# Letting the first output store of a batched matrix product go early, while the next ones stay held back

## The chip, the cores and the metric

The kernel runs on one core of one Trainium2 chip. The metric is device time in microseconds (us). All runs told here are of the state called fast, and each comparison is with runs of the kernel before on the same chip. The profile's span is some 1.8 us shorter than the time of the same execution (124.2 and 125.98 us before); the times in the profile count from the start of that span.

## The reference

Sixteen independent products of 512 x 512 matrices in float32, the second one transposed:

```python
a: (16, 512, 512) float32      b: (16, 512, 512) float32
out = np.matmul(a, b.transpose(0, 2, 1))
```

Inputs are 33.55 MB and the output is 16.78 MB, 50.33 MB in all.

## The kernel before

The batches go in eight pairs. Load `n` brings one operand of a pair (2.1 MB): even `n` are `a`, odd ones `b`, so pair `u` needs loads `2u` and `2u + 1`. VectorE casts the operands to bfloat16, TensorE transposes and multiplies them, ScalarE copies the products from PSUM, into which TensorE writes them, to one of seven output slots. A store writes one batch (1.05 MB). SyncE issues all loads and stores 8 to 15 on its DMA queue (q1 in the profile); GpSimd issues stores 0 to 7 on its own (q0).

```python
STORES = "SSSSOSOSOSSOOOOOO"      # GpSimd's program: S a store, O an output slot freed
LATE = {11: (8, 9), 13: (10, 11), 15: (12, 13)}   # SyncE: stores issued after load n is passed on
...
def landed(n):
    return s_st[n], 16

def store(n):
    engine = nc.gpsimd if n < STORES.count("S") else nc.sync
    engine.wait_ge(s_out, n + 1)                  # batch n has been copied
    engine.dma_start(
        out[n].rearrange("(p j) n -> p j n", j=J), ob[:, n % NO]
    ).then_inc(s_st[n], 16)
...
store(batch - 2)                                  # SyncE, the last two
store(batch - 1)
...
n_st = n_of = 0
nc.gpsimd.wait_ge(s_ld[0], 32)                    # the hold: load 7 has landed
for what in STORES:
    if what == "S":
        store(n_st)
        n_st += 1
    else:
        nc.gpsimd.wait_ge(*landed(n_of)).then_inc(s_of, 1)
        n_of += 1
```

Load 7 uses the same buffer as load 0, and its landing brings `s_ld[0]` to 32. Until then GpSimd issues no store, although batch 0 has been copied long before. (ScalarE signals a pair's first batch together with its first copy of the second one, here at 25.6 us.) An `O` waits until a store has landed and tells ScalarE that its slot may be written again.

## Time and profile before

| what | value |
|---|---|
| time, median of three runs | 125.95 us |
| span of the profile | 124.2 us |
| bytes moved | 50.33 MB |
| busy: TensorE, VectorE, ScalarE | 74%, 56%, 55% of the span |
| DMA: q1 (SyncE), q0 (GpSimd) | 80.2%, 16.0% of 16 engines' span |
| store 0: batch signalled as copied, issued, landed | 25.6, 43.2, 55.3 us |
| last copy ends, last store lands | 114.3, 122.7 us |

No compute engine is busy for much over three quarters of the time, while the 16 DMA engines together are busy for 96% of it. In the profile's slice view each digit is the busy share of one fortieth of the span in tenths, and the GB/s row beneath gives what the DMA moved in it.

### The profile page before, as it was taken

The page shows a single profiled execution, that of the slowest core. Times are in us where ns is not written, and L with a number is a line of the kernel's source. Part 1 is how long each engine was busy: PE and PEld are TensorE (multiplying, and loading weights), DVE is VectorE, ACT ScalarE, POOL GpSimd, SP SyncE. Part 2 cuts the span into 40 slices and gives each one's busy share as a digit, 9 for nine tenths or more (in the row PEclk, how much of TensorE's full clock was granted, in tenths as well). Part 3 has the DMA queues.
Part 4 walks back from the last instruction along what each step waited for, and adds up shares of the span by engine and source line. Part 5 has one row for each costly group of instructions (what it writes and reads, how often), then busy time and mean ns, then how long its engine had stood idle before and what let it go on. Part 6 is the DMA issues. An engine that isn't in the chain of part 4 may idle for free. (4 is left out here: it accounts for less than half of the span.)

```text
span 124.2 us, 2416 instructions
## 1 busy us (share of the span) xinstructions
PE 92.5 (74%) x768; PEld 58.0 (47%) x768; DVE 70.0 (56%) x112; ACT 68.1 (55%) x130; POOL 6.2 (5%) x14
## 2 busy tenths in 40 slices
PE   0006299998999899899989998995699937995000
PEld 0005296467447644764575477343684426541000
DVE  0055676948992897589488578903968059400000
ACT  4005133679558946966695589435665196556000
POOL 2000000000000070002010220000000000000000
PEclk9999999999999999999999999999779999999965
DMA  4999999999999999999999999999999999999970
GB/s 84 401 425 430 443 438 428 433 428 422 428 428 428 428 438 420 401 430 430 414 425 433 430 438 417 435 435 412 454 414 433 409 430 425 430 430 425 428 327 8
DMA packets 4896, 50.33 MB, mean 405 GB/s; under 512 B 544, under 2 KB 544, under 8 KB 544
## 3 DMA queue, kind: packets, MB, share of 16 engines
q1 hardware_dynamic: 3744, 41.94, 80.2%
q0 software_dynamic: 1152, 8.39, 16.0%
HBM read 33.55 MB, written 16.78 MB: 405 GB/s over the span
## 5 line engine op out<-in xcount | busy, mean ns | idle before, releaser
L266 PE MATMUL ps<-tb,ta 128*128 128x512 bf16 x256 | 57.8, 379 | 0.4
L224 ACT COPY ob<-ps 128x512 f32 x64 | 34.4, 589 | 29.7 <-PE ps L266 26.6
L206 ACT COPY ta<-tp 128x512 bf16<-128x512 bf16 x64 | 32.9, 610 | 15.4 <-PE tp L247 15.4
L266 PEld LDWEIGHTS ps<-tb,ta 128*128 128x128 bf16 x256 | 24.2, 98 | 30.5 <-issue 3.9
L247 PE MATMUL tp<-ident,ha 128*128 128x128 bf16 x256 | 20.2, 236 | 12.6 <-PEq L148 12.6
L247 PE MATMUL tp<-ident,hb 128*128 128x128 bf16 x256 | 19.4, 236 | 8.1 <-PEq L148 7.9
L247 PEld LDWEIGHTS tp<-ident,ha 128*128 128x128 bf16 x256 | 17.5, 107 | 15.8 <-issue 14.1
L187 DVE COPY tb<-tp 128x1024 bf16<-128x1024 bf16 x32 | 21.3, 684 | 5.4 <-DVEq L148 5.3
L247 PEld LDWEIGHTS tp<-ident,hb 128*128 128x128 bf16 x256 | 17.2, 107 | 8.7 <-issue 8.7
L167 DVE CAST hb<-ld 128x1024 bf16 x8 | 5.5, 688 | 12.5 <-DVEq L148 12.3
L182 DVE COPY ha<-wa 128x2048 bf16<-128x2048 bf16 x8 | 5.5, 694 | 10.3 <-DVEq L148 10.1
L167 DVE CAST ha<-ld 128x1024 bf16 x8 | 5.5, 687 | 6.6 <-DVEq L148 6.5
L113 POOL DMA_DIRECT2D out_dram<-ob x8 | 5.5, 693 | 65.0 <-DMA ld<-in_b_dram 41.5
L172 DVE CAST hb<-ld 128x1024 bf16 x8 | 5.5, 685 | 1.1 <-DVEq L148 1.1
L172 DVE CAST ha<-ld 128x1024 bf16 x8 | 5.5, 688 | 1.0 <-DVEq L148 1.0
L186 DVE COPY hb<-wb 128x2048 bf16<-128x2048 bf16 x8 | 5.5, 685 | 0.5 <-DVEq L148 0.5
L170 DVE CAST wa<-ld 128x1024 bf16 x8 | 5.5, 686 | 0.0
L170 DVE CAST wb<-ld 128x1024 bf16 x8 | 5.5, 685 | 0.0
L175 DVE CAST wa<-ld 128x1024 bf16 x8 | 5.5, 684 | 0.0
L175 DVE CAST wb<-ld 128x1024 bf16 x8 | 5.5, 682 | 0.0
L197 ACT ACT_TABLE_LOAD x1 | 1.3, 1283 | 1.1 <-SPq L43 1.1
L80 POOL TENSOR_SCALAR_AFFINE_SELECT ident<-ident 128x128 bf16<-128x128 bf16 x1 | 0.3, 283 | 0.2 <-POOL ident L78 0.2
(6 smaller groups left out, 0.8 us busy)
## 6 DMA issues: line engine op xcount, KB each, us to landing
ld<-in_a_dram SPq DMA_DIRECT2D x7, 2048.0 KB, 29.9
ld<-in_b_dram SPq DMA_DIRECT2D x7, 2048.0 KB, 31.1
out_dram<-ob POOLq DMA_DIRECT2D x8, 1024.0 KB, 28.7
out_dram<-ob SPq DMA_DIRECT2D x8, 1024.0 KB, 20.4
ld<-in_a_dram SPq DMA_DIRECT2D x2, 1024.0 KB, 6.2
ld<-in_b_dram SPq DMA_DIRECT2D x2, 1024.0 KB, 10.2
```

Source lines behind the costliest of these rows:

```text
L113: engine.dma_start(out[n].rearrange("(p j) n -> p j n", j=J), ob[:, n % NO]).then_inc(s_st[n], 16)
L167: nc.vector.tensor_copy(out=h[:, :J, :], in_=src[:, :J, :HK]).then_inc(s_cd, 1)
L170: nc.vector.tensor_copy(out=w[:, :J, :], in_=src[:, :J, HK:])
L172: nc.vector.tensor_copy(out=h[:, J:, :], in_=src[:, J:, :HK]).then_inc(s_c, 1)
L175: nc.vector.tensor_copy(out=w[:, J:, :], in_=src[:, J:, HK:]).then_inc(s_w, 1)
L182: nc.vector.tensor_copy(out=ha[:], in_=wa[:]).then_inc(s_ca, 1)
L186: nc.vector.tensor_copy(out=hb[:], in_=wb[:]).then_inc(s_cb, 1)
L187: nc.vector.tensor_copy(out=tb[:, ko, :], in_=tp[:, 2 + ko % 2].rearrange("k j p -> k (j p)"),).then_inc(s_eb, 1)
L206: c = nc.scalar.copy(out=ta[:, ko, e * J * P:(e + 1) * J * P].rearrange("k (j p h) -> k j p h", j=J, h=2), in_=tp[:, ko % 2, :, e * HP:(e ...
L224: c = nc.scalar.copy(out=dst[:, j, :].rearrange("m (p j) -> m p j", j=2 * J), in_=ps[:, j, :].rearrange("m (j p) -> m p j", j=2 * J),)
L247: t = nc.tensor.transpose(tp[:, 2 * x + g, j, :], h[:, j, g * P:(g + 1) * P], ident[:])
L266: t = nc.tensor.matmul(ps[:, j, :], ta[:, ko, (e * J + j) * P:(e * J + j + 1) * P], tb[:, ko, :].rearrange("k (j p) -> k j p", j=2 * J)[:, ...
```

## The change

The intent is to use the time between 25.6 and 43.2 us, in which batch 0 lies finished: its store is issued at once, so its slot comes free sooner and one store less is left for later. The hold stays for the others.

```diff
         n_st = n_of = 0
-        nc.gpsimd.wait_ge(s_ld[0], 32)
         for what in STORES:
+            if n_st == 1 and what == "S":
+                nc.gpsimd.wait_ge(s_ld[0], 32)
             if what == "S":
                 store(n_st)
                 n_st += 1
```

## The prediction

> **What bounds the kernel now.** I began with the page's slice view, because the kernel moves much data for its arithmetic (50.33 MB).
>
> ```profile
> PE   0006299998999899899989998995699937995000
> DMA  4999999999999999999999999999999999999970
> GB/s 84 401 425 430 443 438 428 433 428 422 428 428 428 428 438 420 401 430 430 414 425 433 430 438 417 435 435 412 454 414 433 409 430 425 430 430 425 428 327 8
> q1 hardware_dynamic: 3744, 41.94, 80.2%
> q0 software_dynamic: 1152, 8.39, 16.0%
> ```
>
> From the second slice to the last but one the 16 DMA engines are full, and each of those slices (3.1 us) moves 400 to 450 GB/s. TensorE has weak slices near the start and in the last third; the DMA row has none. The two queue lines say who uses it: SyncE's q1 carries all loads (33.55 MB) and stores 8 to 15, GpSimd's q0 carries stores 0 to 7. At 427 GB/s the 50.33 MB take 117.9 us; the packets run from 1.95 us to 122.28 us, 120.3 us, so only some 2.5 us of that is ramp and ending. The rest of the 125.95 us is a start of 2 us, landing and end of 1.9 us, and 1.75 us by which the timed median exceeds the profiled span of 124.2 us.
>
> Next I read the table of windows, cut where the traffic changes its kind:
>
> ```profile
> 5.00:26.00 21.00, 13.09 (x92) 9.45 (x93) 14.08 (x22) 7.22 (x14) 0.00 (x0) 1.00 1.02 432
> 26.00:43.00 17.00, 15.96 (x167) 10.77 (x166) 11.60 (x20) 13.22 (x27) 0.00 (x0) 1.00 1.01 428
> 47.00:100.00 53.00, 48.90 (x412) 30.20 (x410) 34.04 (x55) 34.06 (x66) 2.86 (x4) 0.97 1.00 426
> 105.00:114.30 9.30, 8.30 (x52) 3.88 (x49) 1.91 (x4) 6.16 (x12) 0.00 (x0) 1.00 1.01 425
> ```
>
> The last column is GB/s, the one before it the DMA share. Loads alone (the first two lines) get 428 to 432, loads mixed with stores 426, stores alone 425. So the order of the same bytes hardly matters to the rate, and there is no idle stretch that an early store could fill.
>
> The page's own last chain names TensorE and ScalarE (it ends with the copy at 113.70 us), but 8 us of DMA follow it, and that is a queue that was already full: SyncE's q1 works off stores 8 to 15 one after the other, landing at 105.12, 107.78, 110.32, 112.85, 115.35, 117.80, 120.26 and 122.74 us (times of the semaphores in the trace), one per 2.5 us, which is 1.05 MB at 427 GB/s.
>
> Last the waits and the order of time:
>
> ```profile
> POOL out_dram L113 <- DMA ld<-in_b_dram: 41.5, 1, 41.5
> POOL out_dram L113 <- DMA out_dram<-ob: 23.5, 3, 10.0
> ...
> 25.05 1.07 ACT L224 COPY ob<-ps 128x512 f32 x2 [0.69 <-PE ps L266]
> 43.21 2.65 POOL L113 DMA_DIRECT2D out_dram<-ob  x4 [41.53 <-DMA ld<-in_b_dram]
> 55.91 0.85 POOL L113 DMA_DIRECT2D out_dram<-ob  x1 [10.04 <-DMA out_dram<-ob]
> ...
> 70.76 0.69 DVE L167 CAST hb<-ld 128x1024 bf16 x1 [1.41 <-DVEq L148]
> 85.06 2.05 ACT L224 COPY ob<-ps 128x512 f32 x4 [3.14 <-ACTq L148]
> 85.68 0.69 DVE L167 CAST hb<-ld 128x1024 bf16 x1 [4.80 <-DVEq L148]
> 100.58 0.69 DVE L167 CAST hb<-ld 128x1024 bf16 x1 [4.84 <-DVEq L148]
> 113.19 1.09 ACT L224 COPY ob<-ps 128x512 f32 x2 [0.60 <-PE ps L266]
> ```
>
> GpSimd's 41.5 us are the hold that the change lifts for one store: batch 0 is complete with the first copy of the pair at 25.05 us, so at 25.6 us, yet the four stores are issued from 43.21 us. The three DVE lines are casts that start within 0.33 us after their load landed (loads 11, 13 and 15 at 70.43, 85.35 and 100.25 us): from pair 5 on, compute follows the loads. The ScalarE line waits 3.14 us for an output slot, freed when store 4 landed at 84.75 us.
>
> **What the Trainium skill says.** "HBM Reference", section Specifications: a core streaming alone measures about 425 GB/s, bounded by its 16 DMA engines. The trace agrees, 425 to 432. "DMA: Bandwidth & Descriptors", section "Queues, rings and completion order": each engine takes its queues in turn, a packet at a time. The trace agrees: between 60 and 90 us q0 moved 4.30 MB (143 GB/s) and q1 8.56 MB (285 GB/s), one to two, and the packets are 8,192 bytes for stores and 16,384 for loads. "SBUF — State Buffer", section "SBUF: two separate sides": a VectorE operation in a two-port mode keeps GpSimd from writing the descriptors of its DMAs. The trace fits but doesn't prove it: from 43.21 us to q0's first packet at 47.00 us passed 3.8 us, and VectorE was busy in all of the 4.00 us from 43 to 47.
>
> **The change part by part.**
>
> *Removed and added:* no instruction of an engine and no byte. Against before, each engine's order is unchanged but for line numbers; one wait on GpSimd moves from before store 0 to before store 1.
>
> *Store 0 moves.* It is issued at 25.6 us instead of 43.2. With 2 to 3.8 us to the first packet it flows from about 29 us, takes 1.05 MB / 143 = 7.3 us, and lands near 37 us instead of 55.33. In that time 1.05 MB of loads are pushed back: 1.05 / 427 = 2.46 us. Load 5 moves from 33.12 to some 35.2 us, load 6 from 38.02 to 40.5, load 7 from 42.91 to 45.4. Their casts began at 34.73, 43.84 and 46.28 us; only load 5 comes later than its cast (0.5 us), and hb of that pair is wanted by TensorE from 39.27 us, its casts being done at 37.2, so this is hidden.
>
> *The held stores move.* The wait for load 7 now ends at 45.4 us instead of 42.9, so stores 1 to 3 are issued 2.5 us later and q0's next packet comes near 49.2 us instead of 47.0. Store 4 waited for store 0 (55.91 us) and now waits only for batch 4, finished at 48.6 us. q0 then has 7 stores left and stays busy, 7.3 us each: stores 1 to 7 should land near 57.5, 65, 72, 79.5, 87, 94 and 100, instead of 62.77, 70.11, 77.48, 84.75, 92.10, 99.27 and 104.79. Each is 5 us earlier.
>
> *The loads pay for it.* From 50 us on, q0 is ahead of before by 1.05 MB less the 2.2 us of later restart (2.2 x 143 = 0.315 MB), 0.735 MB; while both queues run, a delay d satisfies 427 d = 735 + 143 d (in KB and us), so d = 2.6 us. Load 11 lands near 73.0, load 13 near 87.95. For load 15 the bound is firmer: it can be delayed only by q0's bytes that used to come after it, 0.674 MB by the packet records after 100.25 us, so by 0.674 / 427 = 1.6 us, to 101.8.
>
> *Compute.* The waits for output slots of batches 11 and 13 (the 3.14 us above, and the copy at 99.56 us) fall away, as their stores land 5 us earlier; nothing comes of it, because pairs 5, 6 and 7 then start their hb casts at 73.3, 88.3 and 102.1 us instead of 70.76, 85.68 and 100.58. The final copy ends at 114.28 + 1.6 = 115.9 us.
>
> *The end.* After load 15, q1 holds stores 8 to 15: 8 x 1.05 MB / 427 = 19.6 us, 101.8 + 19.6 = 121.4 us, against 122.28 for the last packet before; the other way round, the total is the same 50.33 MB in one unbroken stream from 1.95 us, which gives 122.3 us again. The two differ by what ramp and round-off allow; I take the second. Sum: 0.0 us, provided that store 15 is in the queue in time. Store 14 landed at 120.26, its bytes ended about 119.8, and an issue on SyncE took 1.0 us to its first packet at the start (0.95 to 1.95 us). So store 15 may be issued as late as 118.8 us: slack 4.5 us before (issue at 114.3), 2.9 us after. Store 14: slack 117.3 - 1.0 - 112.1 = 4.2 us before, 2.6 after. No bubble.
>
> **The rivals.**
>
> *Faster because the stores start earlier and the output slots come free.* For it speaks that GpSimd waits 41.5 us and ScalarE 3.14 us. Against it: DMA is full in those very stretches, 428 GB/s from 26 to 43 us, so a store there displaces a load byte for byte. It would need idle DMA time; the end after the last matmul is no such time either. At most it gives a few tenths, 125.5.
>
> *Slower because loads come late to compute and the last stores miss their place.* The delay of up to 2.6 us is real, but slack at the end is 4.2 us and load 15's delay is limited to 1.6. If the whole 2.6 us reached the last copy, there would still be 1.6 us left. To lose 2% (2.5 us) the last copy must slip by 6.7 us. If I have the slack wrong by 2 us, 126.5 to 127.
>
> *A different rate of the mix.* Loads alone 428 to 432, mixed 426: mixed time grows from 57 us to about 58.5, under 1% of 2 us, nothing that one could measure.
>
> **Range and chances.** The stream of bytes and its rate are untouched, so 125.95 stays; I write 125.9. Three runs before lie within 0.08 us; I widen to 125.4 and 126.5 for a small bubble at the end and for another chip's rate. Faster by over 2% would need under 123.4 us, which this DMA rate does not allow: 1%. Slower by over 2% needs the chain of rival two: 3%. Within: 96%.
>
> **What would show it.** Right: DMA row full as before and GB/s unchanged; GpSimd's first store near 25.6 us; its wait of 41.5 us split in two (to 25.6 us for batch 0, then to about 45.4 us for load 7); store 4 near 48.7 us; hb casts of pairs 5 to 7 later by 2.6, 2.6 and 1.6 us; no 3.14 us wait before batch 11; last copy near 115.9 us; span 124.2. Wrong: a slice under 400 GB/s after 110 us (a bubble), a last copy after 118.8 us, or load 15 landing beyond 102.

## The result, and the profile after

The changed kernel took 126.18 us (median of four runs, 126.08 to 126.50) against 125.94 us before. The ratio is 1.0022 with a 95% interval of 1.0005 to 1.004. The change is within 2%, in fact slower by 0.2%, in spite of a store that is issued 17 us earlier. The results are correct.

The slice view of the changed kernel:

```profile
PE   0005299998999899899989986999089993999500
DMA  4999999999999999999999999999999999999890
GB/s 87 398 427 432 448 438 422 432 427 382 403 427 432 438 438 427 422 451 409 424 448 414 435 427 422 453 411 448 416 430 440 416 419 427 422 427 424 337 406 8
```

The DMA row is as full as before, but for one 8 near the end. The GB/s row has two dips that were not there: 382 and 403 in the tenth and eleventh slice (28 to 34 us), and 337 in the thirty-eighth (115 to 118 us). The slice after that one moves 406 where it moved 327 before, so most of what the second dip misses is made up while the other kernel runs out.

The table of windows; the columns are start and end, length, then busy time and number of instructions of TensorE, its weight loads, VectorE, ScalarE and GpSimd, then the granted clock, the DMA share and GB/s:

```profile
26.00:43.00 17.00, 15.96 (x166) 10.76 (x165) 11.51 (x20) 13.23 (x27) 0.65 (x1) 1.00 1.00 417
47.00:100.00 53.00, 46.53 (x391) 28.55 (x390) 34.38 (x55) 33.78 (x65) 3.27 (x6) 0.97 1.01 430
105.00:114.30 9.30, 9.21 (x70) 6.28 (x71) 4.22 (x7) 4.22 (x8) 0.00 (x0) 0.82 1.01 425
```

The first line lost 11 GB/s against 428 before, which is 0.19 MB over 17 us; the second gained 4 GB/s, 0.21 MB over 53 us. By 111 us the same number of bytes has passed in both kernels to within 0.01 MB (46.24 MB by the packet records). The granted clock, the share of TensorE's full clock that it was given, was 1.00 in the last line before; it matters below.

The waits of GpSimd:

```profile
POOL out_dram L113 <- ACT ob L225: 25.6, 2, 24.3
POOL out_dram L113 <- DMA ld<-in_b_dram: 19.0, 1, 19.0
POOL out_dram L113 <- DMA out_dram<-ob: 15.6, 2, 9.1
```

The one wait of 41.5 us is now two, 24.3 us for the copy of batch 0 and 19.0 us for load 7, and the waits for landed stores fell from 23.5 to 15.6 us. In order of time:

```profile
25.98 0.67 POOL L113 DMA_DIRECT2D out_dram<-ob  x1 [24.30 <-ACT ob L225]
45.65 2.05 POOL L113 DMA_DIRECT2D out_dram<-ob  x3 [19.00 <-DMA ld<-in_b_dram]
48.98 0.53 POOL L113 DMA_DIRECT2D out_dram<-ob  x1 [1.28 <-ACT ob L225]
...
73.06 0.69 DVE L168 CAST hb<-ld 128x1024 bf16 x1 [3.61 <-DVEq L149]
87.99 0.69 DVE L168 CAST hb<-ld 128x1024 bf16 x1 [4.84 <-DVEq L149]
102.86 0.69 DVE L168 CAST hb<-ld 128x1024 bf16 x1 [4.70 <-DVEq L149]
...
116.39 1.09 ACT L225 COPY ob<-ps 128x512 f32 x2 [0.60 <-PE ps L267]
```

Store 0 is issued at 25.98 us, stores 1 to 3 from 45.65 us, store 4 at 48.98 us instead of 55.91. The three casts that follow their loads come 2.3 us later each (70.76, 85.68 and 100.58 before). The last copy ends at 117.5 us instead of 114.3. ScalarE's wait of 3.14 us for an output slot is gone. So everything that waited for stores became earlier, everything that waited for loads became later, and the last store lands at 122.89 us where it landed at 122.74.

### The profile page after: what moved, and what is told of

Same layout as the page of the kernel before. It is cut to its first block, busy times and chain, and to the rows that moved or that the text cites. A ratio compares the mean times of both kernels' runs of the same rounds, so it can differ in the third digit from the quotient of the medians.

```text
span 124.3 us, 2416 instructions
## 1 busy us (share of the span) xinstructions
PE 94.2 (76%) x768; PEld 59.4 (48%) x768; DVE 70.5 (57%) x112; ACT 68.3 (55%) x130; POOL 6.0 (5%) x14
## 5 line engine op out<-in xcount | busy, mean ns | idle before, releaser
L248 PE MATMUL tp<-ident,hb 128*128 128x128 bf16 x256 | 20.2, 241 | 9.9 <-PEq L149 9.8
L248 PEld LDWEIGHTS tp<-ident,hb 128*128 128x128 bf16 x256 | 17.9, 110 | 10.8 <-issue 10.8
L113 POOL DMA_DIRECT2D out_dram<-ob x8 | 5.3, 664 | 60.2 <-ACT ob L225 25.6
```

What stands on the lines that cost most here:

```text
L113: engine.dma_start(out[n].rearrange("(p j) n -> p j n", j=J), ob[:, n % NO]).then_inc(s_st[n], 16)
L248: t = nc.tensor.transpose(tp[:, 2 * x + g, j, :], h[:, j, g * P:(g + 1) * P], ident[:])
```

## The experiments

Two questions remained. First, is the time really that of a stream of bytes whose order does not count, or did a gain (output slots free earlier) and a loss (loads later) cancel by chance? Second, the last copy ends 3.2 us later and the stream has a hole of 0.3 MB: why does this cost so little, and what is the 0.2%?

The windows at the end show where to look. The kernel before:

```profile
115.00:116.00 1.00, 0.00 (x0) 0.00 (x0) 0.00 (x0) 0.00 (x0) 0.00 (x0) 1.00 1.01 426
116.00:117.00 1.00, 0.00 (x0) 0.00 (x0) 0.00 (x0) 0.00 (x0) 0.00 (x0) 1.00 1.04 442
...
120.00:121.00 1.00, 0.00 (x0) 0.00 (x0) 0.00 (x0) 0.00 (x0) 0.00 (x0) 0.50 0.34 139
121.00:122.50 1.50, 0.00 (x0) 0.00 (x0) 0.00 (x0) 0.00 (x0) 0.00 (x0) 0.50 0.05 22
```

The changed kernel:

```profile
115.00:116.00 1.00, 1.00 (x6) 0.49 (x5) 0.00 (x0) 0.79 (x2) 0.00 (x0) 1.00 0.49 205
116.00:117.00 1.00, 0.69 (x4) 0.10 (x1) 0.00 (x0) 0.61 (x2) 0.00 (x0) 1.00 0.94 393
...
120.00:121.00 1.00, 0.00 (x0) 0.00 (x0) 0.00 (x0) 0.00 (x0) 0.00 (x0) 0.50 1.05 434
121.00:122.50 1.50, 0.00 (x0) 0.00 (x0) 0.00 (x0) 0.00 (x0) 0.00 (x0) 0.50 0.07 27
```

Before, the full rate ends in the 121st microsecond, and then 22 GB/s remain for more than a microsecond. In the packet records the last five packets are one chain, each starting where the one before ended, from 120.70 to 122.27 us, 0.31 us for 8,192 bytes, which is 26 GB/s: a sixteenth of 427. One DMA engine of the 16, called the straggler below, is behind the others, and the kernel waits for it. In the changed kernel the other 15 engines end near 121.3 instead of 120.7 us, still before the straggler. This gave the theory for the experiments: the end is set by the one engine that has most left to do, and the other 15 have about 1.6 us to spare.

### The dip at the end alone

The kernel before, with its last two stores issued as late as the changed kernel issues them:

```diff
+        nc.sync.wait_ge(*landed(batch - 4))
         store(batch - 2)
+        nc.sync.wait_ge(*landed(batch - 3))
         store(batch - 1)
```

> The kernel before, with stores 14 and 15 issued late by hand: store 14 after store 12 has landed (about 115.4 us instead of 112.1), store 15 after store 13 has landed (about 117.9 instead of 114.3), which is where the changed kernel issues them. Nothing else changes, loads and early stores stay. Theory (the end is set by the one DMA engine with the most left to do; it is busy with store 13 until about 117.5 us, so it never runs out): a dip in GB/s at 115 to 118 us as in the changed kernel, and a ratio to before of 0.999 to 1.001. Rival (the dip is what costs the changed kernel its 0.24 us): ratio 1.0015 to 1.003.

Measured: 126.11 us against 126.04, ratio 0.9999 (0.9987 to 1.0012). The stores were issued at 115.42 and 117.87 us (115.33 and 117.50 in the changed kernel), and the dip was there, 332 GB/s in the same slice. The last store landed at 122.80 us. So a hole of 0.3 MB near the end costs nothing by itself that these runs can tell (at most 0.12%); the theory's expectation was met, and the rival's was not. One thing to keep: the last copy of this run ended at 115.3 us, 1.0 us later than before, although its loads came as before. The granted clock was 0.80 between 100.35 and 107 us.

### Store 0 early, the loads at the end as before

```diff
             if n_st == 1 and what == "S":
-                nc.gpsimd.wait_ge(s_ld[0], 32)
+                nc.gpsimd.wait_ge(s_ld[1], 32)      # load 8
```

> The changed kernel, with stores 1 to 7 held until load 8 has landed (about 50 us) rather than load 7, so that GpSimd's queue is back near its pace of before while store 0 stays early. Load 15 should land near 100.5 us and the last copy end near 114.5. No dip at 115 to 118 us, the dip at 28 to 34 us stays. Theory: ratio to before 0.999 to 1.003; if the 0.24 us came from the dip at the end, 0.999 to 1.001; if from the dip when store 0 starts at 29 us, 1.0015 to 1.003.

Measured: 125.98 against 126.04 us, ratio 0.9998 (0.9985 to 1.0011). Load 15 landed at 99.98 us, the last copy ended at 115.3, the dip near 29 us was there (380 GB/s in its slice) and that at 115 us was not. The dip where store 0 starts costs nothing by itself either, to within 0.11%.

### No hold at all

```diff
         n_st = n_of = 0
-        nc.gpsimd.wait_ge(s_ld[0], 32)
         for what in STORES:
```

> No hold at all: stores 0 to 3 go as they are copied (25.6, 27.8, 37.1, 39.3 us), stores 0 to 7 are done near 88 us. Load 11 about 79 us, load 13 about 92, load 15 about 102.5 (it cannot be later than all eight early stores make it), last copy about 118.6. Theory (one stream of the same bytes, the order does not count): ratio 1.000 to 1.006, with a deeper dip after 115 us. Rival (early stores gain by freeing output slots, late loads lose, and they cancelled by chance in the changed kernel): a clear change, over 1% either way.

Measured: 126.24 against 126.04 us, ratio 1.0022 (1.0009 to 1.0035). Store 7 landed at 88.89 instead of 104.79 us, load 11 at 79.96, load 13 at 92.65, load 15 at 102.43 us, the last copy ended at 118.2 us. Load 11 came over 9 us late, output slots came free up to 18 us sooner (store 0 landed at 37.56 instead of 55.33 us), and the time is the same as that of the changed kernel. A chance cancelling of gain and loss would not have held here too. This is one line of its windows, in the hole at the end:

```profile
115.80:116.60 0.80, 0.80 (x5) 0.34 (x4) 0.00 (x0) 0.72 (x2) 0.00 (x0) 1.00 0.08 31
```

For 0.8 us the DMA moved 31 GB/s: 15 engines had run dry and the straggler worked on. In the packet records the rest end at 122.05 us and the straggler at 122.46, a gap of 0.4 us against 1.6 before: most that the 15 had to spare was used up, and the end moved by 0.2 us.

### Store 15 too late for the straggler too

The kernel before, with the last store behind the landing of the one before it:

```diff
         store(batch - 2)
+        nc.sync.wait_ge(*landed(batch - 2))
         store(batch - 1)
```

> The kernel before, with store 15 issued only when store 14 has landed (about 120.3 us instead of 114.3), 1.5 us past the 118.8 us up to which the prediction says it may be late. Theory (the stream now has a hole at the end on every engine): 1.2 to 2.4 us longer, ratio 1.010 to 1.019. If the end were set by something other than the stream of stores: ratio 1.000 to 1.003.

Measured: 127.31 against 126.04 us, ratio 1.0102 (1.0087 to 1.0117), 1.27 us. Two of its windows:

```profile
118.40:119.40 1.00, 0.00 (x0) 0.00 (x0) 0.00 (x0) 0.00 (x0) 0.00 (x0) 0.50 0.06 25
119.70:120.60 0.90, 0.00 (x0) 0.00 (x0) 0.00 (x0) 0.00 (x0) 0.00 (x0) 0.50 0.00 0
```

First one engine works alone, then none. Store 15 was issued at 120.09 us and its first packet ran at 120.92; the straggler's last packet of store 14 ended at 119.6. So the straggler idled 1.3 us, and 1.27 us is what the kernel lost, though the other 15 had idled from about 118.1 us, 2.8 us long. The loss is the straggler's idle time.

### Half of the early store left out

Wrong, as half of batch 0 is never written:

```diff
+            cols = slice(0, J if n else J // 2)
             engine.dma_start(
-                out[n].rearrange("(p j) n -> p j n", j=J), ob[:, n % NO]
+                out[n].rearrange("(p j) n -> p j n", j=J)[:, cols], ob[:, n % NO, cols]
             ).then_inc(s_st[n], 16)
```

> Wrong on purpose: the changed kernel with only half of batch 0 stored, 0.52 MB less, so half of the early store is missing from the result. Theory (the time is the stream's bytes over 427 GB/s): 1.0 to 1.3 us shorter than the changed kernel, ratio to before 0.991 to 0.995. Rival (compute or the output slots set the end): ratio 1.000 to 1.003 as in the changed kernel.

Measured: 124.74 against 125.92 us, ratio 0.991 (0.9894 to 0.9926). Against before it gained 1.18 us; 0.52 MB over 427 GB/s is 1.23 us. (The changed kernel took 126.18 us, 1.44 us more, somewhat above what I expected. It was run at another time. The dip at 29 us was nearly gone here, 0.03 MB lost from 28 to 35 us instead of 0.17.) Taking half a store away does what moving a whole one does not.

### Leaving one engine out of the last store, and a control

If one engine is behind, a version that gives it less would beat both kernels. By the Trainium skill ("DMA: Bandwidth & Descriptors", section "Why a DMA increments its semaphore by 16 and not by 1") a transfer is spread over the largest number of engines up to 16 that divides its partitions, and SyncE's queue takes the lowest-numbered ones. So store 15 was cut into 120 and 8 partitions:

```diff
-            engine.dma_start(out[n]..., ob[:, n % NO]).then_inc(s_st[n], 16)
+            for lo, hi in ((0, 120), (120, P)) if n == batch - 1 else ((0, P),):
+                engine.dma_start(dst[lo:hi], ob[lo:hi, n % NO]).then_inc(s_st[n], 16)
```

(shortened; the wait for store 15 became one for 32.)

> The kernel before, with store 15 alone cut into partitions 0 to 119 and 120 to 127. By the Trainium skill a transfer of 120 partitions runs on 15 of the 16 DMA engines and one of 8 partitions on the first 8, so the last engine gets nothing of store 15. In the trace of before one engine has work left alone from 120.7 to 122.3 us (27 GB/s and less, a sixteenth of 427). Theory: if that is the engine left out, the stream ends near 120.9 us, 1.0 to 1.5 us sooner, ratio 0.988 to 0.993. If the slow engine is another, or the end is not set by one engine: ratio 1.000 to 1.004 (the first 8 engines get 8 KB more).

> The changed kernel with the same cut of store 15. The other engines lost 0.3 MB (0.7 us) in the dip at 115 to 118 us, and that should now count: 0.5 to 1.0 us sooner than before, ratio 0.992 to 0.996, and 0.4 to 0.8 us later than the same cut in the kernel before. If the dip costs nothing even so, the two cuts are equal. If the cut misses the slow engine: ratio 1.002 to 1.006.

> Control: the kernel before with store 15 cut into partitions 0 to 63 and 64 to 127, both of which run on all 16 engines, four rows each. Every engine has as much to do as before, so ratio 0.999 to 1.002. A gain here would say that cutting itself helps, and not the engine left out.

Measured: the cut in the kernel before 126.33 us (ratio 1.0034, 1.0019 to 1.005), in the changed kernel 126.57 us (1.0064, 1.0032 to 1.0097; single runs up to 127.72), both against 125.92; the control with two halves 125.90 us (0.9999, 0.9985 to 1.0012). The cut missed. The trace agrees with the page in that the semaphore of store 15 took 25 increments instead of the control's 32: 15 and 8 from the engines and, before any of the data, one early step for each piece (115.40 and 115.93 us). In the trace of the first, a chain of single packets still stands at the end: one engine ends the first piece at 122.86 us, over 1 us after the others, and has one packet more, to 123.17 us. Its two increments came last, at 123.27 and 123.56 us. That fits a straggler that is among the engines which got the second piece too, and not the one left out. Which engine it is, the trace does not say.

The cut has an effect of its own besides. In the traces of the three kernels with a cut store, some packets of 8,192 bytes after 118.8 us take about twice the usual 0.31 us (over 0.5 us: 16 in the control, 8 in the cut of the kernel before, 72 in that of the changed kernel, whose profiled run of 127.58 us was one of its two longest). After 105 us, the ten traces without a cut have none. Why is not shown. The comparison that the two cuts were meant to give (does the hole count once the straggler is out of the way?) is therefore inconclusive, and no version that beats the kernel before came of it.

### Where the 0.2% is from

Each dip alone cost nothing that could be measured, but the changed kernel has both, and late loads besides. Three more runs were meant to separate these: both dips without late loads (the edits of the first two experiments together), late loads without store 0 at 29 us, and the changed kernel again. The edit of the second:

```diff
         n_st = n_of = 0
-        nc.gpsimd.wait_ge(s_ld[0], 32)
+        nc.gpsimd.wait_ge(s_ld[6], 16)      # load 6
```

> Both dips of the changed kernel together, without its late loads: store 0 early and stores 1 to 7 held until load 8 has landed (as in hold8), and stores 14 and 15 issued late by hand (as in tail). If the changed kernel's 0.24 us is the two dips together: ratio to before 1.0015 to 1.003. If it belongs to the late loads, or is nothing: 0.999 to 1.001.

> The kernel before, with all stores held until load 6 has landed (38 us) instead of load 7: no store at 29 us, but GpSimd's queue is ahead by 0.7 MB for the rest, as in the changed kernel, so load 15 should land near 102 us and the last copy end near 116 to 117.5, with a dip after 115 us. If the 0.24 us belongs to the late loads: ratio 1.0015 to 1.003. If it needs store 0 at 29 us: 0.999 to 1.001.

> The changed kernel once more beside before, on the same chip as the two others: is the 0.24 us there again? If it is real: ratio 1.001 to 1.004. If it was chance or the chip: 0.999 to 1.001.

Measured, against 125.90 us: both dips 126.17 us, ratio 1.0020 (1.0006 to 1.0035); late loads 126.06 us, ratio 1.0004 (0.999 to 1.0018); the changed kernel 126.27 us, ratio 1.0026 (1.0011 to 1.0041). In the second, load 15 landed at 102.46 us, as late as in the changed kernel (102.53), the last copy ended at 116.5 us, and no dip at 115 us followed, so my expectation of a dip there failed; that makes it the cleaner test of late loads. The 0.2% is real. By the medians it comes with both dips together, but this is not shown. The interval for late loads reaches 1.0018 and overlaps with that for both dips, and the spans of the timed runs (listed to 0.1 us) average 124.12 us before, 124.22 with late loads, 124.26 with both dips and 124.42 in the changed kernel, as if each gave a part. The single profiles even point the other way: the straggler's last packet ends at 122.27 us before, 122.26 with both dips, 122.38 with late loads and 122.41 in the changed kernel.

## Why the prediction was right or wrong

**The main step, "0.0 us", held.** The time is that of one stream of bytes, and an early store displaces loads. Four placings of the same early stores (load 6, load 7, the change, none) lie within 0.3%, while half a store taken away gained 0.9%.

**The moves of stores and loads were right in kind and nearly in size.** Store 0 was issued at 25.98 us (predicted 25.6) and landed at 38.36 (near 37). Load 7 landed at 45.35 us (45.4), load 11 at 72.73 (73.0), load 13 at 87.66 (87.95). Stores 1 to 7 landed from 58.01 to 102.73 us, 2 to 5 us earlier than before, where 5 us was predicted for each: q0 took 7.45 us for each store rather than 7.3. The waits for slots vanished and nothing came of it, as predicted.

**The firm bound for load 15 was wrong.** It was to land by 101.8 us and landed at 102.53. The bound took the stream as unbroken and the engines as equal. But a load has landed only when the slowest engine has its part, and the others were meanwhile ahead: when load 15 landed, 0.69 MB of stores 8 and later had already passed, against 0.40 MB before (packet records, less loads and q0's bytes). The difference over 427 GB/s is 0.7 us, which is the miss.

**The last copy was 1.6 us later than predicted** (117.5, not 115.9). Load 15 accounts for 0.7. The rest is in the stage between the cast of the last operand and the last matmuls. The window of that stage before, and then after:

```profile
100.58:106.22 5.64, 3.00 (x49) 2.74 (x49) 5.12 (x9) 4.44 (x11) 0.00 (x0) 1.00 1.02 427
```

```profile
102.86:109.41 6.55, 4.42 (x50) 4.18 (x49) 5.21 (x9) 3.87 (x8) 0.00 (x0) 0.74 1.01 425
```

The same transposes took 0.9 us longer at a granted clock of 0.74 instead of 1.00. The later run of the changed kernel shows it again (0.73). But this is not something that the change does: the runs of the sections on the dip at the end, on load 8 and on the late store 15, whose load 15 landed within 0.3 us of before, show 0.80 to 0.81 there and a last copy at 115.3 instead of 114.3 us. With late loads but no store at 29 us it was 1.00 in that stage, and the last copy ended 1 us sooner. I had no step for the clock.

**"No bubble" failed.** The slice of 337 GB/s is the sign that I had named for it. The slack of 2.6 and 2.9 us was reckoned from landings, which tell of the slowest engine: a store's semaphore gets 16 increments, and store 13 landed with its last at 117.95 us, but its first, from the fastest engine, came at 115.76. For 15 engines the queue was empty at about 115.5 us; store 14, issued at 115.33, brought its first packets 0.8 us later. It was issued 1.6 us later than predicted, and the 0.9 us of the clock decided it here: with late loads and the clock at 1.00, store 14 was issued at 114.35 us and no dip followed.

**It was still harmless, for a reason that I did not have.** The engines that ran dry are not the one that ends last. I had taken the last 1.6 us of the stream as ramp and ending. They are one engine's backlog, and they are the slack in which the two dips hide. That the predicted time held although a bubble came was luck to this extent. The run that issued store 15 at 120.09 us shows the other side: only the idle time of the straggler counted.

**The rivals.** The faster way did not come: no slot freed early helped. The slower way was there as a mechanism, but it took the spare time of 15 engines and not the end's.

**What stays open.** The two dips together took 0.48 MB in the changed kernel's trace (0.17 from 28 to 35 us and 0.31 from 115 to 121, against 428 GB/s) and 0.50 MB in the run made of both; over 427 GB/s that is 1.1 and 1.2 us, which is under the 1.6 us that the other engines had to spare. The profile of the run made of both shows the last store landing at 122.74 us, exactly as before, although its runs took 0.2% longer. So neither is it shown what the 0.2% is from, nor why the start of q0 at 29 us makes a dip at all, or why the clock fell where it did. Why the straggler falls behind is open too, but the increments tell when it does. In the kernel before, the last of the 16 came 0.14 us after the fifteenth at load 5, with loads alone; with stores on q0 besides, 0.40 us at load 11 and 1.02 us at load 15; and 1.71 us at store 13.

## What to carry to other kernels

When the DMA engines are full from start to end, moving a transfer earlier only moves another one later; look for fewer bytes, or for the engine that ends last. A transfer's landing time is that of the slowest of 16 engines, so reckon slack at the end from the first increment of its semaphore and from the last, which differed by 2 us here. A dip in bandwidth is not yet a loss: ask whether the engine that ends last was in it.

## What the Trainium skill lacked or had wrong

- "DMA: Bandwidth & Descriptors", section "Why a DMA increments its semaphore by 16 and not by 1", says that the engines finish independently, but no page tells how far apart they get in a full stream; section "Latency and other measured facts" says only that engines 7 and 15 are usually slower than the others. By the page's choice of engines, the cut above spared engine 15 and gave engine 7 a packet more, so it could not have helped if the straggler was engine 7. No run here tells which it was. Here the first and last increments of one store were 2.1 us apart (120.60 and 122.74 us), and the last 1.57 us of the stream were one engine alone.
- The same page, section "Latency and other measured facts", gives about 1 us to the first byte for DMAs that GpSimd issues. Here, with the DMA engines full, it was 3.8 to 4.3 us from issue to first packet in each of 13 bursts in nine runs (43.21 to 47.00 us before; 25.98 to 29.77 and 45.65 to 49.57 in the changed kernel; 43.31 to 47.63 in the first experiment). For SyncE's DMAs it gives about 0.6 us, and 0.83 us was measured with the queue empty (120.09 to 120.92).
- "SBUF — State Buffer", section "SBUF: two separate sides": the prediction read the 3.8 us as GpSimd kept from its descriptors by VectorE. In the changed kernel VectorE was idle for 2.16 us of the 3.79 us after 25.98, and it took just as long, so these runs do not bear that reading out. They do not test the page's rule itself.
